# A two-layer decoder trunk on one core: two FFN chunks of layer 0 in seven products instead of eight, partial sums that stay in PSUM over a block boundary, a reordered opening of the FFN, and six row sums moved ahead

## The chip, the cores and the metric

The kernel runs on one core of a Trainium2 chip. The metric is the device time of one execution in microseconds; the profile's span goes from the first to the last instruction of one profiled execution. The engines are called PE (TensorE, matmuls; PEld is its weight load), DVE (VectorE), ACT (ScalarE), POOL (GpSimd) and SP (SyncE, which issues most transfers). Matmul results accumulate in PSUM, in eight banks of 128 x 512 floats.

## The reference, cut to what matters

The trunk has two layers over 256 tokens and 2048 channels in float32. Layer 0 mixes tokens by causal pooling, layer 1 by latent attention with 16 heads; each mixing is followed by a SwiGLU FFN with an inner width of 5632. Every sub-layer is normed, shifted, scaled and gated by vectors computed from `c`.

```python
for i in range(DEPTH):
    shift_m, scale_m, gate_m, shift_f, scale_f, gate_f = jnp.split(sc @ mod_w[i] + mod_b[i], N_MOD, axis=-1)
    ...
    x = x + gate_m[:, None, :] * y
    h = modulate(rmsnorm(x, norm_ffn[i]), shift_f, scale_f)
    x = x + gate_f[:, None, :] * swiglu(h, ffn_gate[i], ffn_up[i], ffn_down[i])

def swiglu(h, w_gate, w_up, w_down):
    return (jax.nn.silu(h @ w_gate) * (h @ w_up)) @ w_down
```

## The kernel before, in words

**Matmuls in three parts.** PE multiplies in a float32 form of less than full precision, so each operand is split into an upper half and a lower half (the rest), and a product is upper x upper + upper x lower + lower x upper. A weight tile is 512 channels by 512 columns (1 MB). `w_unit` (L389) loads one into a `raw` buffer over SP's queue; `split` (L375) makes the upper half on ACT (L380) and the lower half on DVE (L382); `proj_unit` (L397) issues the 3 parts x 4 blocks of 128 channels x 2 halves of the tokens = 24 matmuls of 128 x 512 (L405). Such a tile with its matmuls is a unit here. There are 6 `raw` buffers, 6 `hl` tiles (three pairs of halves), 8 large `act` tiles, 7 small `t2k` tiles and one `gate` tile.

**The FFN.** The 2048 channels of the hidden state are four blocks (hT[0] to hT[3]), the 5632 inner columns are eleven chunks of 512. For a chunk ("p" in `FFN_STEPS`, L59) gate and up each take four units, silu and the product make a tile of 256 tokens x 512, and it is transposed ("t"), on PE (`transposed`, L791) or, for the chunks in `TURNED_BY_DMA`, by DVE in blocks of 32 (L557) and by a write to DRAM and back on POOL's queue. Four groups of chunks (`GROUPS`) are then multiplied with the down weights ("d", `down`, L925), 12 units for three chunks, and the results are added up in x.

**Begun chunks.** Block j+1 of the hidden state isn't there when block j is. So `start_ffn` (L1072) runs chunks 0 to 5 over block 0, then 1, then 2 (three block stages; the first chunks of block 0 are in the opening), while the next block is prepared. Chunk 0 keeps its sums in PSUM (`held`); for the others `Begun.gather` (L733) copies a block's sums out (ACT, L737) or adds them to the earlier ones (DVE, L739). The last block is in the chunk's own step.

**Seven products.** In layer 1 chunks 6 to 10 (`SEVEN`) treat the first two channel blocks, the two halves of the tokens and the pair gate, up as 2 x 2 matrices of tiles and form their product in seven multiplications (`project_in_seven`, L847; matmuls at L867) of sums and differences of tiles. Differences of weight tiles are formed by `minus` (L876) on DVE in the raw buffers, before they are split. The four sums of hidden tiles are formed once per layer by `token_sums` (L808), called at the start of the first down group, and lie in an `act` and in the `gate` tile. Its parts wait in `pending`, the list of follow-up work that `flush` (L361) issues behind each split. Blocks 2 and 3 are done as usual.

**Row sums in the background.** The shift, scale and gate vectors of later steps are products of one row with a large matrix. `Part.unit` loads a 1 MB raw tile and multiplies and sums each row on DVE (L221). These units are queued in `background`; `tick` issues them at a rate set by `plan` (L354), units left over by a count of splits (`FFN0_UNITS`). In the block stages `start_ffn` pumps eight per stage. Weights in `project_in_seven` don't tick. The gate row of each FFN goes through DRAM and is spread to all partitions by POOL (L302), for layer 0 into the single `gate` tile as soon as it can; `StreamEnd.known` (L641) multiplies the sums so far with it in chunk 10's step.

**The opening.** Layer 0's vectors are needed at once and come from strip matmuls on PE (L248), one raw of 1 MB per unit, the last four from `in_mod_block`. Between them an order written out by hand (`then(n, f)`, from `n_block - 1`) sums the squares (`norm_sums`, L1235), spreads the norm (L1266), transposes the mixed stream back (`turn_of`, L1249; matmuls L1253), and picks the columns (`block.fold`, L266). The FFN's first products (L1342) follow.

The order outside the hand-written part comes from a planner that works by priority in program order; splits have priority over what stands up to 100 instructions ahead of them, and a tile is given out when its last user is done.

Of the kernel before, what the change touches and what calls it, by code (L numbers as in the profile page):

```python
# [17 lines left out]
P = 128  # L18
# [40 lines left out]
FFN_STEPS = "p0 p1 t0 p2 t1 p3 t2 p4 p5 d0 t3 t4 p6 t5 d1 p7 t6 p8 t7 p9 t8 d2 p10 t9 d3".split()  # L59
# [3 lines left out]
SEVEN = (range(0), range(6, 11))  # L63

AM, GM = 1, 2
# [4 lines left out]
LATE_GATES = ("ffn1",)  # L70
# [4 lines left out]
FFN0_UNITS, MLA_UNITS, DQ_UNITS, WO_UNITS, FFN1_UNITS = 87, 4, 6, 8, 60  # L75
DOWN_UNITS = 23

# [29 lines left out]
def tile_trunk(ctx: ExitStack, tc: tile.TileContext, a: dict, out: bass.AP):  # L107
# [176 lines left out]
    def gate_to(name, first):  # L284
# [15 lines left out]
        def load():  # L300
            gates[name] = s_row if name in LATE_GATES else gate_t([P, D])
            pool.dma_start(gates[name], row.rearrange("k q -> (k q)")[None, :].to_broadcast([P, D]))  # L302
# [324 lines left out]
    class StreamEnd:  # L627
# [13 lines left out]
        def known(self, j, tok, gate):  # L641
# [3 lines left out]
            if self.l == 0:  # L645
                dve.tensor_tensor(out=piece, in0=piece, in1=gate[:, js], op=ALU.mult)
# [71 lines left out]
    class Begun:  # L718
        def __init__(self, w, c, held):
            self.w, self.c, self.held, self.part = w[:, c], c, held, None  # L720

        def block(self, j, t_):
            if not self.held or j == 0:
                self.banks = [ps_t() for _ in range(NT)]
            hi, lo = w_unit(self.w[j])
            ends = not self.held
            proj_unit(self.banks, t_, hi, lo, ends or j == 0, ends or j == ND - 1)
            if not self.held:
                pending.append((0, lambda banks=self.banks: self.gather(banks, j)))
# [3 lines left out]
        def gather(self, banks, j):  # L733
            for tok in range(NT):
                part = self.part[:, tok, :]
                if j == 0:
                    act.activation(part, banks[tok], AF.Copy)  # L737
                else:
                    dve.tensor_tensor(out=part, in0=banks[tok], in1=part, op=ALU.add)  # L739
# [15 lines left out]
    def ffn(l, hT, gate_name, begun, then):  # L755
# [169 lines left out]
        def down(i):  # L925
            g = GROUPS[i]
            last = g[-1] == NF - 1
            if i == 0 and len(SEVEN[l]):
                release(0, DOWN_UNITS)
# [5 lines left out]
            for j in range(ND):  # L935
# [34 lines left out]
                for tok in range(NT):  # L970
                    if last:
                        pending.append((0, lambda bank=banks[tok], tok=tok, j=j: end.piece(bank, tok, j)))
                    else:
                        pending.append((0, lambda bank=banks[tok], sums=x[:, tok, js]: gather(bank, sums, i == 0)))
                        if gate_name in LATE_GATES and i == len(GROUPS) - 2:
# [3 lines left out]
        def project_chunk(c):  # L979
            if c == ASIDE:  # L980
                stream_aside(l)
            if c == NF - 1:
                end = StreamEnd(l)
                stream_end.append(end)
                for n, wait in enumerate(KNOWN):
                    pending.append((wait, lambda n=n: end.known(n // NT, n % NT, gates[gate_name])))
            if c in SEVEN[l]:
                nat[c] = project_in_seven(c)
                if c == GROUPS[-1][0]:
# [81 lines left out]

    def start_ffn(l, first, ahead, hidden, late):  # L1072
# [7 lines left out]
        with tc.issue_after(mod_ins[0].ins), tc.issue_after(hid_ins[0].ins) if hid_ins[0] else nullcontext():  # L1080
            for j in range(ND - 1):
# [4 lines left out]
                for n, (c, which) in enumerate((c, w) for c in begun for w in (GATE, UP)):  # L1086
                    if n == 2 * len(begun) - 1:
                        hT.append(hidden(j + 1, pieces))
                    if j > 0 or c >= (PAIRS if l == 0 else 1):
                        begun[c][which].block(j, hT[j])  # L1090
# [967 lines left out]
```

## Time and profile before

| | us |
|---|---|
| median of 3 runs | 1870.96 (1869.87 to 1871.59) |
| the profiled execution | 1871.2 |
| its span | 1869.4 |
| mean granted clock of PE | 0.987 |

In the profile a line such as `L405 PE MATMUL ...` is a group of instructions: source line, engine, operation, operands, count, busy time, the mean time of one in ns, and the idle time in front of them with what ended it. A row of the view by windows gives the stretch, its length, and for PE, PEld, DVE, ACT and POOL the busy time and the number of instructions, then the granted clock of PE as a share of full speed, the share of time in which the transfer engines were busy, and GB/s. The chain of waits gives start, length and what ran. A line of the timeline gives start, length, engine, line and operation, and in brackets the idle time in front with its releaser.

### The profile page before, as it was taken

Reading aid. Unit: us, or ns where it says so; the run is one execution under the profiler, and the core shown is the slowest. Engines: PE = TensorE matmul, PEld = TensorE weight load, DVE = VectorE, ACT = ScalarE, POOL = GpSimd, SP = SyncE. Lnnn points to the kernel's source line nnn. Section 1 sums busy time; section 2 is a strip of 40 time slices with the busy share of each in tenths; the row PEclk is TensorE's granted clock in tenths of the full one; section 3 lists DMA queues with packets and bytes.
Section 4 is the critical chain, followed back from the end, with each engine's and each line's share of the span. In section 5 each row is a group of like instructions: output and inputs, shape, how many; then the busy total and the mean of one; then the engine's idle time right before and its main releaser. Section 6 shows DMA issues by size and latency. Waiting matters only on the chain.

```text
span 1869.4 us, 21684 instructions
## 1 busy us (share of the span) xinstructions
PE 1821.3 (97%) x8497; PEld 1481.9 (79%) x8497; DVE 1552.1 (83%) x1552; ACT 879.4 (47%) x955; POOL 68.1 (4%) x98
## 2 busy tenths in 40 slices
PE   7779999999999999999999999999999999999998
PEld 2447888888888888888889888888888888887886
DVE  2467899999889798997798885889899887898696
ACT  3225643453433343344766735644445553655353
POOL 0000000000000000000100000100011000000000
PEclk8899999999999999999999999999999999999999
DMA  9999998889999899996495394999898587458651
GB/s 392 422 422 420 402 380 335 317 313 365 408 349 421 350 399 391 393 422 234 162 384 197 129 366 172 405 373 340 300 336 331 218 318 289 180 206 320 237 227 46
DMA packets 85192, 592.27 MB, mean 317 GB/s; under 512 B 10033, under 2 KB 10465, under 8 KB 16225
## 3 DMA queue, kind: packets, MB, share of 16 engines
q1 hardware_dynamic: 79202, 570.68, 77.9%
q0 software_dynamic: 5648, 19.93, 2.9%
q8 instruction: 66, 1.08, 0.2%
q10 hardware_dynamic: 240, 0.29, 0.0%
q14 instruction: 36, 0.29, 0.0%
HBM read 576.15 MB, written 14.70 MB: 316 GB/s over the span
## 4 chain that ended last, share of the span: by engine, by line
PE 91%; DMA 5%; DVE 2%; ACT 0%; issue 0%; SPq 0%; POOLq 0%; DVEq 0%; ACTq 0%
PE ps L405 73%; PE ps L867 4%; PE ps L415 2%; DMA raw<-in_mod_shift_dram 1%; DMA raw<-in_mod_gate_dram 1%; PE ps L248 1%; PE ps L1657 1%; PE ps L1342 1%; DMA raw<-in_mod_scale_dram 1%; DMA act<-in_pool_w_dram 1%; DVE hl L382 1%; PE ps L1743 1%; PE ps L1849 1%; DMA raw<-in_mod_block_dram 1%; PE ps L1560 1%; PE ps L1746 0%
## 5 line engine op out<-in xcount | busy, mean ns | idle before, releaser
L405 PE MATMUL ps<-hl,act 128*128 128x512 f32 x6096 | 1391.2, 389 | 0.4 <-DVE act L773 0.2
L405 PEld LDWEIGHTS ps<-hl,act 128*128 128x128 f32 x6096 | 1142.7, 188 | 238.6 <-DVE act L773 0.6
L380 ACT ACTIVATE hl<-raw 128x2048 fp32r<-128x2048 f32 x297 | 566.9, 1917 | 570.2 <-PE ps L405 279.0
L382 DVE TENSOR_TENSOR hl<-raw,hl 128x2048 fp32r<-128x2048 f32 x297 | 677.0, 2287 | 107.0 <-ACT hl L380 106.5
L221 DVE SCALAR_TENSOR_TENSOR raw<-raw,s_row 128x2048 f32<-128x2048 f32 x184 | 419.7, 2287 | 0.7 <-DMA raw<-in_mod_wt_dram 0.7
L248 PE MATMUL ps<-raw,s_strip 128*32 128x512 f32 x320 | 49.5, 710 | 28.6 <-DMA raw<-in_mod_shift_dram 16.7
L739 DVE TENSOR_TENSOR act<-ps,act 128x512 f32<-128x512 f32 x96 | 64.2, 685 | 10.2 <-PE ps L405 10.1
L867 PE MATMUL ps<-hl,act 128*128 128x512 f32 x300 | 71.6, 390 | 0.0
L867 PEld LDWEIGHTS ps<-hl,act 128*128 128x128 f32 x300 | 56.2, 188 | 11.9 <-DVE hl L382 0.2
L248 PEld LDWEIGHTS ps<-raw,s_strip 128*32 128x32 f32 x320 | 7.5, 117 | 53.1 <-issue 19.4
L415 PE MATMUL ps<-hl,act 128*128 128x512 f32 x192 | 47.6, 401 | 0.6 <-DVE act L511 0.5
L876 DVE TENSOR_TENSOR raw<-raw,raw 128x2048 f32<-128x2048 f32 x20 | 45.7, 2285 | 0.3
L415 PEld LDWEIGHTS ps<-hl,act 128*128 128x128 f32 x192 | 35.1, 188 | 10.3 <-ACT act L498 2.5
L1207 PE MATMUL ps<-act,act 128*128 128x256 f32 x128 | 34.3, 427 | 7.6 <-issue 7.6
L1207 PEld LDWEIGHTS ps<-act,act 128*128 128x128 f32 x128 | 26.9, 215 | 17.5 <-issue 13.3
L559 POOL DMA_DIRECT2D turned<-t2k x32 | 17.8, 555 | 612.6 <-DVE t2k L557 612.4
L435 ACT ACTIVATE junk<-x 128x512 bf16<-128x512 f32 x23 | 14.5, 629 | 45.7 <-DVE x L654 28.6
L528 DVE TENSOR_TENSOR hl<-raw,hl 128x2048 fp32r<-128x2048 f32 (+3 forms) x17 | 31.9, 1879 | 4.8 <-ACT hl L525 4.7
L737 ACT ACTIVATE act<-ps 128x512 f32<-128x512 f32 x32 | 18.9, 594 | 29.8 <-PE ps L405 29.8
L804 DVE TENSOR_TENSOR x<-ps,x 128x512 f32<-128x512 f32 x32 | 21.6, 690 | 12.0 <-PE ps L405 12.0
L867 PE MATMUL ps<-hl,gate 128*128 128x512 f32 x120 | 29.4, 392 | 0.6 <-ACT hl L380 0.6
L525 ACT ACTIVATE hl<-raw 128x2048 fp32r<-128x2048 f32 (+1 forms) x15 | 26.5, 1766 | 3.5 <-PE ps L405 3.5
(275 smaller groups left out, 1203.4 us busy)
## 6 DMA issues: line engine op xcount, KB each, us to landing
raw<-in_mod_wt_dram SPq DMA_DIRECT2D x152, 1024.0 KB, 8.1
raw<-in_ffn_down_dram SPq DMA_DIRECT2D x88, 1024.0 KB, 7.8
raw<-in_ffn_gate_dram SPq DMA_DIRECT2D x86, 1024.0 KB, 6.4
raw<-in_ffn_up_dram SPq DMA_DIRECT2D x86, 1024.0 KB, 6.5
raw<-in_kv_mod_wt_dram SPq DMA_DIRECT2D x32, 1024.0 KB, 8.7
raw<-in_mod_shift_dram SPq DMA_DIRECT2D x16, 1024.0 KB, 12.4
raw<-in_w_o_dram SPq DMA_DIRECT2D x16, 1024.0 KB, 6.6
raw<-in_mod_gate_dram SPq DMA_DIRECT2D x12, 1024.0 KB, 12.5
```

Of the source, the lines that this page charges most:

```text
L221: dve.scalar_tensor_tensor(out=r, in0=r, scalar=1.0, in1=s_row, op0=ALU.mult, op1=ALU.mult, accum_out=self.sums[:, self.n:self.n + 1])
L248: pe.matmul(self.bank[m * STRIP:(m + 1) * STRIP, :], lhsT=s_strip[:, self.kt + k, :], rhs=r[:, k, i, :], start=first, stop=last)
L380: hi_ins = act.activation(hi, r, AF.Copy)
L382: lo_ins = dve.tensor_tensor(out=lo, in0=r, in1=hi.bitcast(F32), op=ALU.subtract)
L405: pe.matmul(banks[tok], lhsT=t_[:, i, k, tok * P:(tok + 1) * P], rhs=w[:, k, :], start=first and n < len(part), stop=last and n >= len(ord ...
L415: pe.matmul(bank, lhsT=t_[:, i, k, tok * P:(tok + 1) * P], rhs=w[:, k, :], start=first and n == 0, stop=last and n == len(order) - 1)
L525: hid_ins[0] = act.activation(w[1], w[0], AF.Copy)
L528: dve.tensor_tensor(out=w[2][:, ks], in0=w[0][:, ks], in1=w[1][:, ks].bitcast(F32), op=ALU.subtract)
L739: dve.tensor_tensor(out=part, in0=banks[tok], in1=part, op=ALU.add)
L867: pe.matmul(bank, lhsT=a_(i, k), rhs=w[:, k, :], start=first and n == 0, stop=last and n == len(order) - 1, skip_group_check=read)
L876: dve.tensor_tensor(out=out, in0=a_, in1=b_, op=ALU.subtract)
L1207: pe.matmul(mixed[g][:, n % 2, :], lhsT=wp[g][:, k, ns], rhs=pool_all[g // 2][:, g % 2, k, :], start=k == 0, stop=k == KL - 1)
```

## The change

1. `SEVEN` gets chunks 6 and 7 of layer 0, so `token_sums` runs in layer 0 too. Its second tile takes the `gate` tile, so layer 0's gate row is loaded late, after chunk 7, and the sums are multiplied with it in the third down group as in layer 1. `FFN0_UNITS` falls from 87 to 71, since two chunks no longer tick.
2. `Begun.block` can leave a chunk's sums in PSUM over a block boundary (`goes_on`), for the chunk that comes last in a stage and first in the next; `visits` sets such orders, and the FFN starts with chunk 1 instead of 0. This holds for both layers.
3. `SOONER = 3`: three more row sums in each of the second and third block stages of layer 0.
4. In the opening the sums of squares get 64 equal columns instead of one, transposes are moved ahead, and nine transposes of the identity are added (`keep_busy`), whose results nobody reads.

```diff
-FFN_STEPS = "p0 p1 t0 p2 t1 p3 t2 p4 p5 d0 t3 t4 p6 t5 d1 p7 t6 p8 t7 p9 t8 d2 p10 t9 d3".split()
+FFN_STEPS = "p1 p0 t1 p2 t0 p3 t2 p4 p5 d0 t3 t4 p6 t5 d1 p7 t6 p8 t7 p9 t8 d2 p10 t9 d3".split()
-SEVEN = (range(0), range(6, 11))
+SEVEN = (range(6, 8), range(6, 11))
+WIDE = 64
-LATE_GATES = ("ffn1",)
+LATE_GATES = ("ffn0", "ffn1")
-FFN0_UNITS, MLA_UNITS, DQ_UNITS, WO_UNITS, FFN1_UNITS = 87, 4, 6, 8, 60
+FFN0_UNITS, MLA_UNITS, DQ_UNITS, WO_UNITS, FFN1_UNITS = 71, 4, 6, 8, 60
+SOONER = 3
...
-            gates[name] = s_row if name in LATE_GATES else gate_t([P, D])
+            gates[name] = s_row if name == "ffn1" else gate_t([P, D])
...
-        def known(self, j, tok, gate):
+        def known(self, j, tok):
             js = slice(j * CH, (j + 1) * CH)
             part, piece = self.parts[tok][:, js], x[:, tok, js]
-            if self.l == 0:
-                dve.tensor_tensor(out=piece, in0=piece, in1=gate[:, js], op=ALU.mult)
             dve.tensor_tensor(out=part, in0=piece, in1=part, op=ALU.add)
...
+            self.banks, self.empty = None, True
-        def block(self, j, t_):
-            if not self.held or j == 0:
+        def block(self, j, t_, goes_on=False):
+            first, ends = self.banks is None, j == ND - 1 or not (self.held or goes_on)
+            if first:
                 self.banks = [ps_t() for _ in range(NT)]
             hi, lo = w_unit(self.w[j])
-            ends = not self.held
-            proj_unit(self.banks, t_, hi, lo, ends or j == 0, ends or j == ND - 1)
-            if not self.held:
-                pending.append((0, lambda banks=self.banks: self.gather(banks, j)))
+            proj_unit(self.banks, t_, hi, lo, first, ends)
+            if ends and not self.held:
+                pending.append((0, self.gather))
                 if j == ND - 1:
                     flush()
-        def gather(self, banks, j):
+        def gather(self):
             for tok in range(NT):
                 part = self.part[:, tok, :]
-                if j == 0:
+                if self.empty:
-                    act.activation(part, banks[tok], AF.Copy)
+                    act.activation(part, self.banks[tok], AF.Copy)
                 else:
-                    dve.tensor_tensor(out=part, in0=banks[tok], in1=part, op=ALU.add)
+                    dve.tensor_tensor(out=part, in0=self.banks[tok], in1=part, op=ALU.add)
+            self.banks, self.empty = None, False
...
-            if i == 0 and len(SEVEN[l]):
-                release(0, DOWN_UNITS)
+            if i == 0:
+                if l == DEPTH - 1:
+                    release(0, DOWN_UNITS)
                 token_sums()
...
-                        if gate_name in LATE_GATES and i == len(GROUPS) - 2:
+                        if i == len(GROUPS) - 2:
...
-                if c == GROUPS[-1][0]:
+                if c == min(SEVEN[l][-1], GROUPS[-1][0]):
                     late_gates.pop()()
...
+    def visits(j, n):
+        return ([*range(n)], [n - 1, *range(3, n - 1), 0, 1, 2], [*range(2, n), 0, 1])[j]
...
                 todo = KD // 2 if j + 1 >= ND - late else 0
-                for n, (c, which) in enumerate((c, w) for c in begun for w in (GATE, UP)):
+                if l == 0 and j > 0:
+                    todo += SOONER
+                for n, (c, which) in enumerate((c, w) for c in visits(j, len(begun)) for w in (GATE, UP)):
...
-                        begun[c][which].block(j, hT[j])
+                        begun[c][which].block(j, hT[j], n >= 2 * len(begun) - 2)
...
-                    pe.matmul(total[:, tok:tok + 1], lhsT=squares[n][:, k, tok * P:(tok + 1) * P], rhs=ones[:, 0:1],
+                    pe.matmul(sums_wide[:, tok, :], lhsT=squares[n][:, k, tok * P:(tok + 1) * P], rhs=ones[:, :WIDE],
                               start=n + tok + k == 0, stop=n + tok + k == 4)
...
+    def keep_busy(n):
+        for _ in range(n):
+            pe.transpose(total[:, :P], ident, ident)
...
     then(n_block, norm_sums, (1, 2))
+    then(n_block, turn_of, ORDER[1])
     then(n_block, lambda: pairs[1].split_upper())
     then(n_block, turned_copies)
     then(n_block, norm_rows)
     then(n_block, lambda: pairs[1].split_lower())
-    then(n_block + 1, turn_back, ORDER[1])
     then(n_block + 1, norm_spread)
     then(n_block + 1, parts_of_first)
-    then(n_block + 2, turn_back, ORDER[2])
-    then(n_block + 3, turn_of, last, (0,))
+    then(n_block + 1, turn_back, ORDER[2])
+    then(n_block + 2, turn_of, last, (0,))
+    then(n_block + 2, keep_busy, 4)
+    then(n_block + 3, turn_of, last, (1,))
     then(n_block + 3, block.fold)
-    then(n_block + 3, turn_of, last, (1,))
+    then(n_block + 3, keep_busy, 5)
```

## The prediction on record

> **What bounds the kernel now.** I read the page first, then the chain of waits in order of time, then the busy time by stage.
>
> ```profile
> span 1869.4 us, 21684 instructions
> PE 1821.3 (97%) x8497; PEld 1481.9 (79%) x8497; DVE 1552.1 (83%) x1552; ACT 879.4 (47%) x955; POOL 68.1 (4%) x98
> DVE  2467899999889798997798885889899887898696
> DMA  9999998889999899996495394999898587458651
> PE 91%; DMA 5%; DVE 2%; ACT 0%; issue 0%; SPq 0%; POOLq 0%; DVEq 0%; ACTq 0%
> L405 PE MATMUL ps<-hl,act 128*128 128x512 f32 x6096 | 1391.2, 389 | 0.4 <-DVE act L773 0.2
> L382 DVE TENSOR_TENSOR hl<-raw,hl 128x2048 fp32r<-128x2048 f32 x297 | 677.0, 2287 | 107.0 <-ACT hl L380 106.5
> L221 DVE SCALAR_TENSOR_TENSOR raw<-raw,s_row 128x2048 f32<-128x2048 f32 x184 | 419.7, 2287 | 0.7 <-DMA raw<-in_mod_wt_dram 0.7
> L739 DVE TENSOR_TENSOR act<-ps,act 128x512 f32<-128x512 f32 x96 | 64.2, 685 | 10.2 <-PE ps L405 10.1
> ```
>
> PE is 91% of the chain that ended last, and its largest group waited 0.4 us in all. So an instruction taken off PE shortens the run, provided the others keep up; a matmul's 389 ns is its latency, since they are pipelined. The 5% of DMA in the chain is the opening. The engine next to the bound is DVE. Its prices are busy time over count: 677.0/297 = 2.28 us for a lower half of a weight tile (L382), 419.7/184 = 2.28 for a row sum (L221), 64.2/96 = 0.67 for a 128x512 add.
>
> **Part 1: fewer products.** Layer 1 of this same kernel already forms chunks 6 to 10 this way, so its chunk 6 shows what the new order costs PE. From the chain of waits, and the busy time of the whole chunk 6 and of chunk 9 in layer 1:
>
> ```profile
> 1478.98 2.72 PE ps L867 x12
> 1481.70 5.44 PE ps L405 x24
> 1479.00:1520.00 41.00, 41.00 (x182) 33.89 (x182) 34.18 (x17) 24.47 (x19) 0.00 (x0) 1.00 0.62 234
> 1667.00:1708.00 41.00, 40.21 (x176) 32.47 (x175) 38.08 (x26) 23.53 (x19) 2.63 (x4) 1.00 0.59 213
> ```
>
> A product is 12 matmuls, 2.72 us. An ordinary chunk has four channel blocks times gate and up times 24 = 192 matmuls; the new order has seven products for the first two blocks, 84, and 96 for the other two: 180. Two chunks save 2 x 2.72 = **5.4 us**, if PE stays fed. The first row of windows says it can be: PE busy 41.00 of 41.00. The second says that it isn't always: DVE is at 38.08 of 41, and PE loses 0.8 us.
>
> **Part 2: the opening.** The chain of waits just before the FFN, with the clock in three windows, the wide-to-be sums, a transfer's landing and the issue of the block strips:
>
> ```profile
> 138.61 12.45 DMA raw<-in_mod_block_dram
> 151.10 1.93 PE ps L248 x8
> 153.03 1.90 PE ps L1253 x8
> 154.93 0.85 PE ps L1266 x2
> 155.78 1.51 PE ps L248 x8
> 157.29 1.02 PE ps L1253 x8
> 158.32 1.04 PE ps L248 x8
> 160.09 1.07 PE ps L266 x8
> 162.09 22.10 PE ps L1342 x96
> 147.22 2.84 PE L1239 MATMUL ps<-ones,t2k 128*128 128x1 f32 x24
> 150.00:152.00 2.00, 0.96 (x9) 0.20 (x8) 1.08 (x4) 1.48 (x3) 0.70 (x1) 0.50 0.98 406
> 154.00:156.00 2.00, 2.00 (x11) 1.26 (x13) 0.18 (x1) 1.20 (x2) 0.00 (x0) 0.50 1.00 418
> 158.00:160.00 2.00, 1.90 (x15) 0.66 (x13) 0.00 (x0) 1.56 (x3) 0.00 (x0) 1.00 1.00 418
> 148.60 1.91 ACT L1325 ACTIVATE hl<-raw 128x2048 fp32r<-128x2048 f32 x1 [0.40 <-DMA raw<-in_ffn_first_dram]
> L236 SPq DMA_DIRECT2D raw<-in_mod_block_dram x4: 328/328/328, 132.8 to 142.7; - x4
> ```
>
> After 24 one-column matmuls and a wait the granted clock is 0.50, and eight strip matmuls take 1.93 us where they take 1.04 at full clock. The change makes the sums 64 columns wide, puts eight transposes (ORDER[1]) into the wait of about 1 us that ends at 151.10, and adds nine transposes as filler. If the clock holds, the three strip units and the transposes between 151.10 and 159.36 shrink from 8.3 us to about 6. What then ends last is a transfer. Strip raws landed at 151.06 (138.61 + 12.45) and a weight raw at 148.60, one megabyte each 2.5 us; the last strip, third from 151.06 counting itself, so lands at 151.06 + 2 x 2.5 = 156.1 (an estimate: landings of the last two aren't shown). It was used at 158.32. Gain 0 to **2.2 us**; I take 2.2, for the DMA queue is full in all three windows (0.98 to 1.00) and its order up to there is unchanged. The 64-column sums cost between nothing (a weight load in 0.118 us, 2.84/24, is there already) and as much again, 2.8; either fits ahead of 156.1, except for what hangs on it on DVE. The filler stands in PE's own waits, 162.09 - 161.16 = 0.9 us after the fold for five transposes.
>
> [...]
>
> **Part 3: DVE and the row sums.** Chunk 5, then 2, then 1 stay in their banks over a block boundary. That takes 3 x 4 adds off DVE in the second and third block stages of layer 0 (chunk 5's first gather, on ACT, falls one stage later). In come six row sums. Later in the FFN DVE gets: six row sums fewer; four times tile sums with halves, 14 operations of 0.67; per chunk three more lower halves, four differences of weight tiles, five adds more. The gate's eight multiplications only move, from chunk 10 to the third down group. The stages before:
>
> ```profile
> 227.80:358.60 130.80, 130.80 (x579) 108.31 (x578) 120.91 (x113) 55.59 (x43) 0.00 (x0) 1.00 0.91 349
> 358.60:842.80 484.20, 484.20 (x2166) 401.19 (x2165) 435.17 (x353) 194.72 (x140) 8.62 (x13) 1.00 0.95 380
> 358.60:426.30 67.70, 67.70 (x312) 56.33 (x311) 65.91 (x65) 32.37 (x31) 0.00 (x0) 1.00 0.83 310
> 426.30:493.50 67.20, 67.20 (x306) 55.68 (x305) 60.54 (x48) 26.89 (x23) 0.71 (x1) 1.00 0.98 398
> 453.57 27.25 PE ps L405 x120
> 454.36 1.92 ACT L380 ACTIVATE hl<-raw 128x2048 fp32r<-128x2048 f32 x1 [0.48 <-ACT t2k L293]
> ```
>
> Second and third block stage: 120.9 + 6 x 2.28 - 12 x 0.67 = 126.6 of 130.8 us, 97%; DMA 349 + 6.3 MB/130.8 us = 397 GB/s. FFN up to the last down group: 435.2 - 13.7 + 14 x 0.67 + 2 x (7 x 2.28 + 5 x 0.67) = 435.2 - 13.7 + 9.4 + 38.6 = 469.5 of 484.2 - 5.4 = 478.8 us, **98%** against 90% before. PE never waits in these rows, so the change can win nothing there beyond the products; it can lose.
>
> Where first? In the first down group (426.3 to 493.5), which had 60.5 of 67.2. The rate of row sums goes from 84/87 to 78/71 a unit, so 12 units carry 1.6 more, 3.6 us; the six chunks before, full at 65.9 of 67.7, push their own 3.6 into it; the tile sums add 9.4. That makes 77.1, 9.9 too many. Two things absorb it. The margin: the upper half made at 454.36 to 456.28 is taken by the second unit from 453.57, at 453.57 + 27.25/5 = 459.0, 2.7 us later (counting units through the ring of three tile pairs). And chunk 6 carries no row sums: 34.2 of 41.0, 6.8 us free into which late row sums can slip, since nobody waits for them soon. The loss is 9.9 - 2.7 = 7.2 if none slips, 0.4 if all does. I take **2.6**: most slips, as row sums are the work that the planner lets fall behind, but each holds one of six raw buffers, which weights then lack, and chunk 9 of layer 1 lost 0.8 at a smaller load.
>
> Costed at nothing: the gate row's load on POOL's queue, now behind chunk 7, lands over 80 us before the third down group uses it, and behind it only stores of turned blocks wait; uncovered it would be one landing. Chunk 1 before chunk 0 and the transposes with them: PE has the same units. Layer 1's changed visits: PE is busy throughout its blocks too. Six row sums' transfers on SP's queue go ahead of weights that the 397 GB/s still leave room for.
>
> Sum, on the profiled execution (1871.2 us, span 1869.4, 1.8 around it): 1871.2 - 5.4 - 2.2 + 2.6 = 1866.2. The median 1870.96 is 0.2 lower: **1866.0 us**. 0.2% of it, about what a measurement can tell from no change, is 3.7 us.
>
> **The rivals.**
> *DVE takes it back.* If few row sums slip, PE loses the full 7.2 there, and perhaps a little again in the third down group, which gains the eight multiplications: 1871.0 - 7.6 + 7.2 = 1870.6, up to 1872. For it: 98% over 479 us; 97% was held for 68 us only. Against it: the surplus of work lies in one place, with slack behind it.
>
> *Tile sums come too late: slower.* They need two t2k tiles at a time; of seven, chunks 3, 4 and 5 hold six until the transposes of chunk 3, at 480.8 in this trace (the 27.25 us from 453.57 end there), one or two units before chunk 6. If they run only then, in front of the lower halves that PE needs, the third product of chunk 6 waits for all 9.4 us of them and for two differences and two lower halves behind, 4 x 2.28 = 9.1: 1871.0 - 7.6 + 9.4 + 9.1 = 1881.9 if none of it is beside PE's work, 1875 with 7 us beside it. It decides from where more than 8.2 + 5.4 us of DVE work (36 matmuls of chunk 6 and the last unit before) stands ahead of that product's tile. Against: only three of the four sums lead to that product, and layer 1 does it without a wait; but there turned chunks go out by DMA early and t2k is free.
>
> *The clock stays down.* Transposes between strips may not hold it, or the strips are too sparse: at 0.50 three strip units take 0.9 us more each than I allow, which eats the 2.2: 1868.2.
>
> **How the numbers follow.** Forecast (1862.5 to 1867.3: all of the 2.2, loss 0 to 4) 0.52; clock stays down 0.12; DVE takes it back 0.18; tile sums late 0.18. That the products aren't fewer is excluded by the list of chunks. Faster than 1867.3: the forecast's 0.52 and 0.03 of the clock's case, 0.55; slower than 1874.7: most of the last, 0.16; same 0.29. The range leaves out the worse half of the last case and little below: 1862 to 1876.
>
> **What would show it.** Right: 24 matmuls fewer over L405 and L867 together; FFN products (L1342) beginning near 160 at clock 1.00 throughout; DVE near 97% from 230 to 840; one or two PE gaps between 430 and 540. Wrong: PE waiting for DVE or ACT by more than 7 us in layer 0; a clock under 1 at 155; PE idle ahead of the first product over a tile sum; or no wait at all, and 1863.

## The result, and the profile after

The changed kernel takes 1886.58 us (median of 5 runs, 1885.54 to 1888.79) against 1870.96 (1869.87 to 1871.59): ratio 1.0086, interval [1.0076, 1.0097]. It is slower by 16 us where 5 were forecast as a gain. From the page of the profiled execution (1888.79 us):

```profile
span 1887.0 us, 21675 instructions
PE 1822.4 (97%) x8482; PEld 1477.3 (78%) x8482; DVE 1581.1 (84%) x1566; ACT 894.6 (47%) x973; POOL 67.8 (4%) x98
PE 83%; DVE 9%; DMA 4%; issue 2%; ACT 1%; POOL 0%; SPq 0%; DVEq 0%; POOLq 0%; ACTq 0%
L408 PE MATMUL ps<-hl,act 128*128 128x512 f32 x5904 | 1356.3, 391 | 8.3 <-ACT hl L383 6.7
L385 DVE TENSOR_TENSOR hl<-raw,hl 128x2048 fp32r<-128x2048 f32 x303 | 688.7, 2284 | 107.0 <-ACT hl L383 106.6
```

L405 of before is L408, L382 is L385, L867 is L870. PE has its fewer matmuls, and its largest group now waits 8.3 us instead of 0.4. DVE's share of the chain has gone from 2% to 9%, and it is there that the chain must be read: most of PE's waits name ACT, whose upper half came late because of DVE. The waits of PE that are new or longer, from the view of waits (what waited for what, in all, how often, the longest):

```profile
PE ps L408 <- ACT hl L383: 6.7, 5, 2.8
PE ps L294 <- DVE cols L308: 2.7, 1, 2.7
PE ps L870 <- ACT hl L383: 1.8, 3, 1.0
PE ps L870 <- DVE gate L822: 1.6, 1, 1.6
PE ps L408 <- DVE hl L385: 1.4, 3, 0.7
```

These are 14.2 us, all but 0.8 of them in layer 0's FFN, and two of the pauses cost more than their length: at 2.72 us for 12 matmuls, those behind 2.67 us (88 in 21.82) took 1.9 us longer, those behind 2.84 us (24 in 8.54) 3.1. Where they are, from PE's timeline (start, length, line, count, and in brackets the wait ahead):

```profile
413.01 5.73 PE L408 MATMUL ps<-hl,act 128*128 128x512 f32 x24 [1.40 <-ACT hl L383]
421.41 0.27 PE L294 MATMUL ps<-con,cols 128*16 128x128 f32 x1 [2.67 <-DVE cols L308]
421.43 21.82 PE L408 MATMUL ps<-hl,act 128*128 128x512 f32 x88
...
500.42 1.91 PE L794 MATMUL ps<-con,t2k 128*128 128x128 f32 x16
502.09 3.12 PE L870 MATMUL ps<-hl,act 128*128 128x512 f32 x12
...
508.04 8.54 PE L408 MATMUL ps<-hl,act 128*128 128x512 f32 x24 [2.84 <-ACT hl L383]
...
520.04 2.12 PE L870 MATMUL ps<-hl,gate 128*128 128x512 f32 x8 [1.55 <-DVE gate L822]
...
618.70 2.88 PE L870 MATMUL ps<-hl,act 128*128 128x512 f32 x12
...
815.54 27.51 PE L408 MATMUL ps<-hl,act 128*128 128x512 f32 x120 [1.99 <-ACT hl L383]
```

Behind the waits of chunk 6, 24 matmuls take 8.54 us, where 24 take 5.44 at full clock: the granted clock is 0.50 from 508 to 514 us. By stage, in the changed kernel and then in the one before (columns as in the prediction):

```profile
358.00:426.00 68.00, 62.95 (x277) 50.15 (x276) 62.87 (x62) 27.09 (x27) 0.00 (x0) 0.97 0.87 332
426.00:493.00 67.00, 66.29 (x293) 54.40 (x292) 64.61 (x50) 27.87 (x21) 0.00 (x0) 1.00 0.96 386
493.00:560.00 67.00, 61.69 (x268) 49.46 (x267) 59.46 (x49) 37.58 (x33) 0.00 (x0) 0.95 0.61 239
```

```profile
358.00:426.00 68.00, 68.00 (x314) 56.56 (x313) 65.90 (x65) 32.67 (x30) 0.00 (x0) 1.00 0.83 311
...
493.00:560.00 67.00, 67.00 (x302) 55.55 (x301) 57.03 (x44) 27.14 (x18) 2.62 (x4) 1.00 0.93 362
```

For all kernels below one length is compared, "the FFN length": from the first FFN products (L1342 before, L1357 after) to the last down products, which a chain of waits shows as 44 matmuls. Before and after:

```profile
877.16 9.98 PE ps L415 x44
```

```profile
161.41 22.10 PE ps L1357 x96
...
894.27 9.98 PE ps L418 x44
```

Before it is 877.16 - 162.09 = 715.1 us, after 894.27 - 161.41 = 732.9. The products take 5.4 off, so 23.2 us are lost in layer 0's FFN; ahead of it the changed profile is 0.7 us quicker, and behind it 0.5 slower. Up to chunk 6's first product it is 502.09 - 161.41 = 340.7 against 493.5 - 162.09 = 331.4, so 9.3 in the begun chunks and the first down group. From there to chunk 7's first product it is 116.6; 180 + 288 matmuls of 2.72/12 us and eight transposes (0.88) make 107.0, so 9.6 in chunk 6. The remaining 4.3 come later: the two longest waits there are 0.96 us in chunk 7 and 1.99 us in chunk 10 (at 815.54), and what makes up the rest stays open.

DVE's own line in chunk 6 shows the cause there (DVE's timeline):

```profile
450.46 0.68 DVE L826 TENSOR_TENSOR t2k<-act,act 128x512 f32<-128x512 f32 x1
...
495.68 0.17 DVE L276 TENSOR_TENSOR cols<-sums,vcol 128x16 f32<-128x16 f32 x1
501.06 0.69 DVE L827 TENSOR_TENSOR t2k<-act,act 128x512 f32<-128x512 f32 x1 [5.21 <-PE ps L794]
501.67 2.28 DVE L385 TENSOR_TENSOR hl<-raw,hl 128x2048 fp32r<-128x2048 f32 x1
```

The first operation of the tile sums runs at 450.46; the second, of the same sum, needs another `t2k` tile, which chunk 3 gives back only at its transposes, at 500.42, now behind all twelve units of the down group. DVE stands idle for 5.21 us, and the lower halves of chunk 6 behind that instruction stand with it.

### The profile page after: what moved, and what is told of

Same layout as the page of the kernel before. It is cut to its first block, busy times and chain, and to the rows that moved or that the text cites. A ratio compares the mean times of both kernels' runs of the same rounds, so it can differ in the third digit from the quotient of the medians.

```text
span 1887.0 us, 21675 instructions
## 1 busy us (share of the span) xinstructions
PE 1822.4 (97%) x8482; PEld 1477.3 (78%) x8482; DVE 1581.1 (84%) x1566; ACT 894.6 (47%) x973; POOL 67.8 (4%) x98
## 4 chain that ended last, share of the span: by engine, by line
PE 83%; DVE 9%; DMA 4%; issue 2%; ACT 1%; POOL 0%; SPq 0%; DVEq 0%; POOLq 0%; ACTq 0%
PE ps L408 64%; PE ps L870 6%; DVE hl L385 4%; DVE raw L224 2%; PE ps L418 2%; DMA raw<-in_mod_shift_dram 1%; DMA raw<-in_mod_wt_dram 1%; PE ps L1357 1%; PE ps L251 1%; DMA raw<-in_mod_scale_dram 1%; PE ps L1675 1%; PE ps L1761 1%; PE ps L1867 1%; DMA raw<-in_mod_gate_dram 1%; ACT hl L383 1%
## 5 line engine op out<-in xcount | busy, mean ns | idle before, releaser
L408 PE MATMUL ps<-hl,act 128*128 128x512 f32 x5904 | 1356.3, 391 | 8.3 <-ACT hl L383 6.7
L408 PEld LDWEIGHTS ps<-hl,act 128*128 128x128 f32 x5904 | 1109.0, 188 | 244.1 <-ACT hl L383 8.8
L383 ACT ACTIVATE hl<-raw 128x2048 fp32r<-128x2048 f32 x303 | 577.5, 1916 | 529.7 <-PE ps L408 225.6
L385 DVE TENSOR_TENSOR hl<-raw,hl 128x2048 fp32r<-128x2048 f32 x303 | 688.7, 2284 | 107.0 <-ACT hl L383 106.6
L870 PE MATMUL ps<-hl,act 128*128 128x512 f32 x420 | 101.4, 391 | 1.0 <-ACT hl L383 1.0
L870 PEld LDWEIGHTS ps<-hl,act 128*128 128x128 f32 x420 | 78.3, 188 | 18.4 <-ACT hl L383 1.4
L879 DVE TENSOR_TENSOR raw<-raw,raw 128x2048 f32<-128x2048 f32 x28 | 63.9, 2284 | 0.4
L741 DVE TENSOR_TENSOR act<-ps,act 128x512 f32<-128x512 f32 x80 | 52.9, 681 | 10.9 <-PE ps L408 10.8
L870 PE MATMUL ps<-hl,gate 128*128 128x512 f32 x168 | 41.8, 395 | 3.1 <-DVE gate L822 1.6
L870 PEld LDWEIGHTS ps<-hl,gate 128*128 128x128 f32 x168 | 31.2, 188 | 11.2 <-DVE gate L822 2.0
```

The costliest lines, as they stand in the source:

```text
L383: hi_ins = act.activation(hi, r, AF.Copy)
L385: lo_ins = dve.tensor_tensor(out=lo, in0=r, in1=hi.bitcast(F32), op=ALU.subtract)
L408: pe.matmul(banks[tok], lhsT=t_[:, i, k, tok * P:(tok + 1) * P], rhs=w[:, k, :], start=first and n < len(part), stop=last and n >= len(ord ...
L741: dve.tensor_tensor(out=part, in0=self.banks[tok], in1=part, op=ALU.add)
L870: pe.matmul(bank, lhsT=a_(i, k), rhs=w[:, k, :], start=first and n == 0, stop=last and n == len(order) - 1, skip_group_check=read)
L879: dve.tensor_tensor(out=out, in0=a_, in1=b_, op=ALU.subtract)
```

## The experiments

Unless it is said otherwise an edit is made to the changed kernel. Ratios are to the kernel before, measured beside each run. The questions come in this order: are the seven products needed for the loss, what holds up chunk 6, what holds up the begun chunks, and can the loss be avoided. "Row sums a unit" means row sums issued per weight tile that ticks.

| run | median us | ratio [95%] | FFN length us |
|---|---|---|---|
| e1_beside | 1869.72 | 0.9995 [0.9986, 1.0005] | 715.1 |
| e2_turned | 1884.22 | 1.0069 [1.0052, 1.0086] | 729.8 |
| e3_early_turn | 1881.33 | 1.0054 [1.0039, 1.0069] | 726.9 |
| e4_half_rows | 1886.12 | 1.0079 [1.0064, 1.0094] | 730.3 |
| f1_sooner | 1878.93 | 1.0040 [1.0026, 1.0054] | 724.7 |
| f2_rate | 1883.65 | 1.0066 [1.0051, 1.0081] | 730.5 |
| f3_both | 1882.39 | 1.0059 [1.0044, 1.0074] | 727.8 |
| f4_early_late | 1884.93 | 1.0072 [1.0057, 1.0087] | 729.7 |
| g1_spread | 1901.82 | 1.0165 [1.0149, 1.0180] | 719.2 |
| g2_one_chunk | 1886.61 | 1.0082 [1.0065, 1.0099] | 714.7 |
| g3_gate_later | 1878.43 | 1.0039 [1.0025, 1.0054] | 724.6 |
| g4_six_ahead | 1910.08 | 1.0209 [1.0193, 1.0224] | 730.0 |
| h1_one_even | 1872.30 | 1.0007 [0.9998, 1.0017] | 718.3 |
| h2_gate_row | 1880.52 | 1.0048 [1.0031, 1.0065] | 727.2 |
| h3_gate_row_only | 1869.62 | 0.9993 [0.9984, 1.0002] | 715.6 |
| h4_two_even | 1880.59 | 1.0052 [1.0037, 1.0067] | 727.4 |
| i2_other_engines | 1973.35 | 1.0551 [1.0529, 1.0573] | - |
| i4_other_engines_plain | 1954.22 | 1.0447 [1.0431, 1.0463] | - |

**Without the seven products, and what they bring along.**

```diff
-SEVEN = (range(6, 8), range(6, 11))
+SEVEN = (range(0), range(6, 11))
-LATE_GATES = ("ffn0", "ffn1")
+LATE_GATES = ("ffn1",)
-FFN0_UNITS, ... = 71, ...
+FFN0_UNITS, ... = 87, ...
-SOONER = 3
+SOONER = 0
```

(and no token sums in layer 0.)

> The changed kernel without the seven products in layer 0 and what goes with them (no tile sums there, gate row loaded early, 87 units, no row sums moved ahead); the opening, the banks kept over a block boundary and the order of chunks stay. All theories that put the loss on the seven products (DVE over-subscribed, tile sums late, raw buffers held) say the same: no PE gap in layer 0 after the opening, and 1870.96 minus the 0.7 us by which the first products came sooner, 1869 to 1871. If the kept banks or the new order of chunks cost something themselves, it is above 1873.

The 16 us are gone, so the opening, the order of visits and the banks kept over a boundary do no harm; the chain of waits has its FFN products early:

```profile
159.71 22.05 PE ps L1358 x96
```

That is 2.4 us sooner than before, in a profiled execution that is 1.0 us below the run's median. The time is no different from before within its interval.

**Chunk 6: who holds the tiles.** Two runs free `t2k` tiles earlier, by turning chunks 3 to 5 by DMA (`TURNED_BY_DMA = (range(3, 9), ...)`), and by a step of its own that transposes chunk 3 into PSUM ahead of the down group:

```diff
-p4 p5 d0 t3 t4 p6
+p4 p5 u3 d0 t3 t4 p6
```

> Chunks 3, 4 and 5 of layer 0 are turned by DVE blocks and transfers as in layer 1, not by PE: their t2k tiles are free early, DVE has six more 128x512 operations (4 us), PE 24 transposes fewer (2.6 us). Tile sums late: chunk 6's loss falls to 1 to 3 us, total 1875 to 1879. DVE over-subscribed: 4 us more for DVE eat what the freed tiles give, 1883 to 1888.

> Chunk 3 is transposed into PSUM before the first down group and copied out after it, so its two t2k tiles are free when the tile sums start; the same instructions on every engine. Tile sums late: chunk 6 loses 1 to 3 us instead of 10, total 1877 to 1880. DVE over-subscribed alone: DVE only gets back the 5.2 us in which it stood behind the transposes, and the sums move into the down group, 1881 to 1885. Raw buffers held: no change, 1885 to 1888.

Windows of the second:

```profile
358.00:426.00 68.00, 62.91 (x277) 50.10 (x276) 64.53 (x64) 28.74 (x28) 0.00 (x0) 0.97 0.86 325
460.00:500.00 40.00, 37.79 (x164) 30.34 (x163) 39.90 (x36) 18.03 (x16) 0.00 (x0) 1.00 0.98 384
500.00:520.00 20.00, 18.62 (x83) 14.46 (x83) 19.90 (x13) 12.37 (x12) 0.00 (x0) 1.00 0.48 186
```

DVE's wait of 5.21 us is gone and 5.2 us of the time with it. From chunk 6's first product (502.68) to chunk 7's (612.08) it is 109.4 us, so chunk 6 loses 2.4 instead of 9.6; but PE now waits 2.2 us for lower halves in the down group, where the sums run. The loss in the begun chunks (62.91 of 68) is untouched: it is another one. The first run, which gives DVE six more operations, wins back 2.4 us: chunk 6 loses less there too (PE 64.50 of 67 from 493 to 560, against 61.69), but the begun chunks and the down group lose more (61.66 of 68, 64.51 of 67).

**Is it DVE's amount of work?** Each background row sum on half of its columns, the other half left out:

```diff
+cs = slice(0, D // 2 if self in background or self.brief else D)
-dve.scalar_tensor_tensor(out=r, in0=r, scalar=1.0, in1=s_row, ...
+dve.scalar_tensor_tensor(out=r[:, cs], in0=r[:, cs], scalar=1.0, in1=s_row[:, cs], ...
```

> Row sums of the background multiply and sum only half of each row (1024 of 2048 columns), so 168 of them cost DVE about 1.2 us instead of 2.3, with the same transfers and raw buffers; the vectors they give are wrong. DVE over-subscribed: the gaps in the six begun chunks go (9 us) and some of chunk 6's, 1873 to 1878. Tile sums late: chunk 6 keeps most of its 10 us, since the wait is for PE's transposes, 1876 to 1880. Raw buffers or transfers: no change, 1885 to 1888.

```profile
358.00:426.00 68.00, 64.32 (x287) 50.74 (x286) 58.18 (x68) 29.67 (x30) 0.00 (x0) 1.00 0.81 308
```

DVE is busy 58.2 us of 68, and PE still loses 3.7. The timeline of DVE there shows why:

```profile
349.72 0.08 DVE L227 DVE_READ_ACCUMULATOR raw<-raw,s_row 128x1 f32 x1
358.49 0.69 DVE L744 TENSOR_TENSOR gate<-ps,gate 128x512 f32<-128x512 f32 x1 [8.68 <-PE ps L411]
359.09 2.28 DVE L388 TENSOR_TENSOR hl<-raw,hl 128x2048 fp32r<-128x2048 f32 x1
```

The waits of PE in this stretch name lower halves of DVE alone (2.4 us), and none a transfer, though the total lies where the rival of raw buffers and transfers had it. DVE waits 8.68 us for PE with an addition (L744 here, L741 in the changed kernel) at the head of its line, and the next lower half, which needs nothing of PE, stands behind it. The number of lower halves ahead of such operations can be read off the program's DVE order: ahead of the up multiplications of the six begun chunks there are 36, 38, 40, 42, 44, 46 before and 34, 36, 38, 41, 43, 45 after. And beside them go 8 row sums before, 11 after. In this run the order is not quite that of the changed kernel (34, 36, 38, 40, 42, 44). In chunk 6 nothing is won at all: DVE stands 7.34 us in front of the second operation of the tile sums, and from 493 to 560 PE has 60.63 us of 67. So the amount of work alone explains neither place.

**What costs it: the six ahead, or the rate?** Three runs on the kernel of the first experiment: `SOONER = 3` alone, `FFN0_UNITS = 76` alone, and `SOONER = 3` with 71.

> The changed kernel without seven products (chunks 6 and 7 as before, early gate row, no token sums), row sums again spread over 87 units, but three more row sums in each of the second and third block stages. Theory L (lead): what PE loses in the six begun chunks is set by how many lower halves stand ahead of each up multiplication in DVE's order. In DVE's program order the first multiplication of the six chunks has 36, 38, 40, 42, 44, 46 lower halves ahead of it before, 34, 36, 38, 41, 43, 45 after, and 35, 36, 38, 41, 43, 46 here: so a part of the loss, 1 to 5 us between 358 and 426, total 1870 to 1875. Rival T (throughput): what counts is DVE's work in that stretch, which here is lower than before (0.90 row sums a unit instead of 0.97): no loss, total 1868 to 1870.

> As the run beside it, but with the six row sums where they were and the row sums at 84 in 76 units, 1.1 a unit like in the changed kernel. Theory L: 36, 37, 39, 42, 43, 46 lower halves ahead of the up multiplications, one fewer than before in three places: 0 to 1.5 us lost between 358 and 426, total 1869 to 1872. Rival T: DVE's work in that stretch rises from 63.7 us by 0.14 x 24 x 2.2 = 7 us above the 68 us there are: 3 to 7 us lost, total 1873 to 1877.

> Both together: six row sums ahead and 1.1 a unit, still no seven products and no token sums. DVE's order up to the end of the six begun chunks is then that of the changed kernel (34, 36, 38, 41, 43, 45 lower halves ahead). Theory L: the changed kernel's whole loss in that stretch, 7 to 10 us, total 1876 to 1880, and no further loss behind it. Rival S (the seven products themselves, through transfers or buffers of chunk 6, hold up the chunks before): no loss, total 1869 to 1871.

PE's timeline in the first and in the second, and the window of the third:

```profile
404.65 19.89 PE L408 MATMUL ps<-hl,act 128*128 128x512 f32 x87
431.85 0.38 PE L294 MATMUL ps<-con,cols 128*16 128x128 f32 x1 [7.32 <-DVE cols L308]
431.88 13.46 PE L408 MATMUL ps<-hl,act 128*128 128x512 f32 x49
```

```profile
445.76 0.27 PE L294 MATMUL ps<-con,cols 128*16 128x128 f32 x1 [3.52 <-DVE cols L308]
445.79 19.57 PE L408 MATMUL ps<-hl,act 128*128 128x512 f32 x78
...
529.07 16.19 PE L408 MATMUL ps<-hl,act 128*128 128x512 f32 x64 [2.54 <-ACT hl L383]
```

```profile
358.00:426.00 68.00, 62.89 (x278) 50.16 (x277) 63.68 (x63) 27.89 (x28) 0.00 (x0) 0.97 0.86 326
```

The third reproduces the loss of the begun chunks without any seven products (62.89 against 62.95), so it isn't theirs; its total is above both ranges, as PE loses another 2.4 us between 680 and 860. The first two went past both theories (and rival T counts 24 units in a stretch of twelve, so its price is twice too high). With the six alone there is one wait, of 7.32 us: `spread` transposes the gate row on PE, for the last of the gate's sixteen row sums, which now falls where DVE is latest; 49 matmuls behind it take 13.46 us instead of 11.1. With the rate alone (1.1 a unit) the begun chunks run full, and the loss follows, mostly between 430 and 760: 15.4 us of the FFN length, more than the 12.7 of both together.

**The gate row.** A first attempt (`pending.append((5, spread))` for `(1, spread)`, on f1_sooner) left layer 0's order as it was, since the list is emptied at the end of each begun chunk; it is a repetition of that run. The second moves one row sum, the gate's last, behind eight of the next vector:

```diff
     kv_part(0, shift_to, C_SKV)
+    background.insert(-8, background.pop(-KD - 1))
```

> The kernel without seven products and with three more row sums in each of two block stages (1878.9), with one edit: the spread of the gate row, a transpose on PE that waited 7.3 us for the last of its row sums, is issued four splits later in PE's order. Theory H (head of the line): the 7.3 us are PE's own order, behind which matmuls stood that were ready; with the transpose later the wait and the slow clock behind it go: 1869 to 1872. Rival: DVE is late as a whole by then, and PE waits instead for lower halves: 1874 to 1879.

> The same move of one row sum in the kernel without seven products and with three more row sums in each of two block stages (1878.9; one wait of 7.3 us and matmuls 2.4 us slower behind it). Theory H: both go, 1869 to 1871. Rival B: PE waits for lower halves instead, 1875 to 1879.

> The changed kernel with chunk 3 turned early (1881.3), and the last of the sixteen row sums of layer 0's gate row done after eight sums of the next vector, so that its transpose on PE comes later. Theory H (a single late sum at the head of PE's line): its wait of 2.7 us and the slow clock behind it go, 1876 to 1879. Rival B (DVE is late as a whole): PE waits elsewhere for as long, 1880 to 1883.

Moved in the kernel with the six ahead (h3_gate_row_only), it takes all of the 9 us away:

```profile
358.00:426.00 68.00, 68.00 (x313) 56.56 (x312) 63.51 (x61) 29.15 (x27) 0.00 (x0) 1.00 0.85 323
```

So, at this rate, the six row sums ahead cost nothing by themselves, nor do the one or two lower halves less ahead. In the changed kernel with chunk 3 turned early, the same move (h2_gate_row) changes next to nothing (1880.52 against 1881.33; FFN length 727.2 against 726.9): the wait of 2.6 us goes, but PE then waits for the halves behind, as a DVE that is late as a whole would have it.

**Fewer row sums a unit.** f4_early_late has chunk 3 turned early and `SOONER = 0` (84 in 71 units, 1.18). Three others spread them thinner. On top of that, g1_spread has `MIX_LATE = 18` (six left to layer 1), two units of each seven-product chunk that tick, and 79 units; g2_one_chunk has one chunk only, `MIX_LATE = 15` and 83 units; g4_six_ahead is g1_spread with `SOONER = 3` and the `(5, spread)` that had no effect in layer 0.

> The changed kernel with seven products in chunks 6 and 7, with chunk 3 turned ahead of the first down group, and with the six row sums left where they were (84 over 71 units). 36, 37, 39, 41, 43, 46 lower halves ahead of the up multiplications. Theory L: of the 8.7 us in the six begun chunks 6 to 8 go, against 1881.3 with the six row sums ahead; behind them the denser row sums (1.18 a unit) cost 0 to 3: total 1873 to 1878. Rival T: the chunks carry 0.08 x 24 x 2.2 = 4 us more of row sums, the loss grows: 1882 to 1886.

> The changed kernel with chunk 3 turned early, the six row sums where they were, six row sums left to layer 1's mixing, the rest spread over four more units at the end of the FFN and four units inside chunks 6 and 7: 78 in 79 units, 0.99 a unit. Theory B (backlog): DVE clears about 0.97 row sums a unit beside the lower halves, as in the kernel before; whatever is issued beyond that stands in front of lower halves and of the gate row's transposes until it has been paid, so at 0.99 the loss goes and the 5.4 us of the products remain: total 1864 to 1869. Rival K: chunks 6 and 7 are too full by themselves (their halves, differences and now two row sums each): 3 to 7 us lost in 500 to 550 and 600 to 660 together, total 1870 to 1875.

> As the run beside it, but only chunk 6 in seven products: 81 row sums in 83 units, 0.98 a unit, three left to layer 1's mixing, none in chunk 6. Theory B: half of the products' gain, no loss: total 1866 to 1869. Rival K: the loss in chunk 6 alone, 2 to 4 us: 1869 to 1872.

> As the first of this call, but with the six row sums ahead in the block stages (72 left in 79 units, 0.91 a unit) and the gate row's transpose four splits later. Theory B: the six are paid in the block stages, which have DVE at 60 to 62 of 66 us, so nothing is lost: 1864 to 1869. Rival L: DVE enters the six begun chunks with one lower half less ahead, which costs 2 to 5 us there: 1867 to 1873.

At 1.18 the begun chunks lose only 1.1 us, but the next 67 us lose 7.3: the loss moved. The first down group of f4_early_late:

```profile
426.00:493.00 67.00, 59.71 (x256) 48.37 (x254) 63.97 (x59) 26.88 (x25) 0.00 (x0) 0.95 0.96 371
```

At 0.99 (g1_spread) PE is full in both stages (68.00 of 68 and 67.00 of 67). With the six ahead at 0.91 a unit (g4_six_ahead) the gate row's wait is back, and it is the only one in these two stages:

```profile
PE ps L294 <- DVE cols L308: 8.2, 1, 8.2
```

The FFN length is 719.2 in g1_spread; with one chunk it is 714.7. These runs are slower as a whole all the same: the row sums left over are then issued in four units of layer 1's mixing, where PE has 25 us of 40, with transfers at 1.00:

```profile
940.00:980.00 40.00, 25.07 (x114) 21.39 (x113) 37.48 (x39) 13.62 (x18) 0.00 (x0) 0.75 1.00 406
```

More were left over than meant: nothing ticks in the last down group (`hold`), so units counted there never came. What g1_spread still loses in the FFN, 719.2 - (715.1 - 5.4) = 9.5 us, lies mostly in chunks 6 and 7, where PE has 37.35 of 40 us and 56.92 of 60: here rival K was right. In chunk 6 (L891 is `minus`, L882 the product; timelines of DVE, ACT and PE):

```profile
499.94 2.29 DVE L891 TENSOR_TENSOR raw<-raw,raw 128x2048 f32<-128x2048 f32 x1
...
502.33 5.52 ACT L383 ACTIVATE hl<-raw 128x2048 fp32r<-128x2048 f32 x3 [5.29 <-DVE raw L891]
...
504.29 2.12 PE L882 MATMUL ps<-hl,act 128*128 128x512 f32 x8 [1.47 <-ACT hl L383]
```

A weight difference is formed on DVE, then its upper half on ACT, then PE has it: in a seven-product chunk what stands ahead in DVE's line delays ACT too.

**Without leaving work to layer 1.** Row sums may run into the first half of the last down group:

```diff
-                if last and j == 0:
+                if last and j == (2 if l == 0 else 0):
                     hold()
```

with one chunk, chunk 3 turned early, `SOONER = 0` and 83 units (h1_one_even), and with both, the gate's sum moved, `SOONER = 3` and 75 units (h4_two_even).

> Only chunk 6 in seven products, chunk 3 turned early, no row sums ahead, nothing left to layer 1: row sums may run on into the first half of the last down group, 84 in 83 units, 1.01 a unit. Theory B (row sums beyond what DVE clears beside the lower halves stand in front of work that PE needs): layer 0's FFN, from its first product to the last down sums, takes 713 to 716 us against 715.1 before, total 1867 to 1871. Rival R (1.01 is already too dense, as 1.1 was): 3 to 8 us more: 1872 to 1877.

> The changed kernel with chunk 3 turned early, the last gate sum moved, and row sums that may run on into the first half of the last down group: 78 in 75 units, 1.04 a unit. Theory B: the loss in the six begun chunks and the first down group falls from about 9 us to 2 to 5: total 1870 to 1876. Rival L (the order at the entry of the begun chunks, 34, 36, 38, 41, 43, 45 lower halves ahead, is unchanged): the loss stays, 1877 to 1881.

One chunk at 1.01 a unit is at the time of before (its FFN 3.2 us longer, the opening 1.8 shorter), so the product it saves is lost again, as rival R had it. Both at 1.04 are 12.3 us longer in the FFN, so they lose 17.7, as much as h2_gate_row: the begun chunks lose less (PE 65.62 of 68 against 63.38), but the last down group, into which row sums now run, loses 3.3 us (36.70 of 40 from 860 to 900). No version beat the kernel before by more than its interval.

**Row sums on other engines.** Every fourth row sum as a multiplication on POOL and a sum on ACT:

```diff
+if self in background and self.n % 4 == 1:
+    pool.tensor_tensor(out=r, in0=r, in1=s_row, op=ALU.mult)
+    act.activation(r, r, AF.Copy, accum_out=self.sums[:, self.n:self.n + 1])
```

> Seven products in chunks 6 and 7, chunk 3 turned early, the last gate sum moved, no row sums ahead, and every fourth row sum formed by a multiplication on POOL and a sum on ACT instead of on DVE: 21 of 84 fewer for DVE, 46 us, of 478. Theory B (DVE's work as such): the loss in the six begun chunks and the first down group goes, chunks 6 and 7 keep 2 to 4 us of theirs: 1866 to 1871. Rival P: a multiplication of 128x2048 on POOL takes long (an estimate from its 128x512 operation of 1.76 us: 7 us), holds its raw buffer and is waited for by ACT, in whose line the upper halves stand: 1876 to 1890.

> The same in the kernel without seven products and without row sums ahead (1869.7), as a control: theory B sees DVE relieved where it was no bound: 1868 to 1871. Rival P: the same waits of ACT for POOL, 1874 to 1890.

The first is 102 us slower than the kernel before, and the control loses most of that too, 83 us; both are far above either expectation. The control's groups, and DVE and POOL side by side:

```profile
L225 POOL TENSOR_TENSOR raw<-raw,s_row 128x2048 f32<-128x2048 f32 x42 | 232.1, 5525 | 767.9 <-DMA raw<-in_mod_wt_dram 527.0 <-DMA raw<-in_kv_mod_wt_dram 112.9 <-DVE soft L1797 59.4
L389 DVE TENSOR_TENSOR hl<-raw,hl 128x2048 fp32r<-128x2048 f32 x297 | 736.5, 2489 | 174.8 <-ACT hl L387 173.2 <-issue 1.2
```

```profile
357.66 5.93 POOL L225 TENSOR_TENSOR raw<-raw,s_row 128x2048 f32<-128x2048 f32 x1 [36.18 <-DMA raw<-in_mod_wt_dram]
...
360.06 7.88 DVE L389 TENSOR_TENSOR hl<-raw,hl 128x2048 fp32r<-128x2048 f32 x2 [0.94 <-ACT hl L387]
```

POOL takes 5.5 us, and the lower halves that meet it here end late: the pair takes 7.88 us, where two took 4.49 in f1_sooner (at 409.40). POOL ends at 363.59, two lower halves of 2.2 later it is 368.0, and the pair ends at 367.94. ACT, in turn, waits 191 us in all for POOL's products, as rival P had it. How the 83 us divide between the two isn't shown. So this is no test of DVE's load, and that question stays open on this side.

## Why the prediction was wrong

**The products: right.** 24 fewer matmuls over L408 and L870, 5.4 us, and chunk 6 in layer 1 at the old pace.

**The opening: about right.** FFN products begin at 161.41 in this profile, and between 159.6 and 161.0 in the experiments, against 162.09: 0.7 to 2.5, forecast 2.2. The clock is 1.00 from 150 to 162 in the windows of the changed kernel and to 160 in those of the first experiment, so the rival that it stays down fell. The fillers didn't bring it up: the first of them starts at 156.97. Whether the wide sums did it alone (24 in 2.89 us, against 2.84 before, so their width cost nothing) or with the transposes moved behind them, no run here separates.

**The step that failed is the loss term of part 3: 2.6 us taken, 23 found in the same FFN.** The amount of work was right: 469.5 us of DVE forecast up to the last down group, and 469.5 busy between 358 and 860 us. What failed is the step from there to PE's loss, that most of the surplus would slip into free time: the stretch took 502 us, not 478.8. Three things in it were wrong.

First, "most slips, as row sums are the work that the planner lets fall behind". The program fixes the order on an engine (in chunk 6 DVE stood 5.21 us in front of one operation, the lower halves behind it), and with 11 row sums instead of 8 beside the begun chunks they stood ahead of lower halves, one or two fewer of which were ready. I let the six begun chunks push their excess on without cost; they cost most of the 9.3 us, the down group, where I had placed the loss, about 1. Shown are: that it comes without seven products (f3_both), that neither of the two causes alone loses anything there but the gate row's wait (h3_gate_row_only, f2_rate up to 426), and that, with the six left in their place, thinning the row sums from 1.18 to 0.99 a unit takes away all that the begun chunks and the first down group lose (8.4 us, f4_early_late against g1_spread). How it divides between amount and order isn't shown: with half the amount, in nearly the same order, 3.7 us were still lost (e4_half_rows).

Second, a row sum that nobody waits for soon: the last one of the gate row is waited for at once, by a transpose in PE's line. That is 2.7 us here and 7.3 in f1_sooner, and no rival had it. Here its removal won nothing clear (h2_gate_row), as PE then waited for lower halves.

Third, the rival "tile sums come too late" came true as described: `t2k` tiles of chunk 3, sums only behind its transposes, 9.6 us lost in chunk 6, where I gave 11.6 to 18.5. Its argument against, that only three of four sums lead to that product, was no help, since DVE waits in the middle of the first. e3_early_turn shows it: with the tiles free, chunk 6 loses 2.4 us, and 5.2 of the whole come back, since the sums then take 2.2 us from the down group. I gave it 0.18 and priced it without the loss before it.

Two smaller errors. Every pause was priced by its length; but matmuls behind some pauses ran at a lower granted clock first: 0.50 from 508 to 514 us, which cost 3.1 us in chunk 6 beside waits of 5.1, and 0.83 from 420 to 440 us in f1_sooner, where 49 matmuls took 2.4 us longer behind the 7.3. And the forecast's lower bound, 1862.5, is 0.9 below what its own terms give (1871.0 - 5.4 - 2.2 = 1863.4).

## What to carry to other kernels

On an engine that is 90% busy, ask of each added instruction what stands behind it in the order, not what share of the time it adds: its margin is the number of finished tiles ahead of the consumer, and two causes that each leave some of it can together take it all. Look for instructions that wait for a buffer or for another engine at the head of a full line, and for small ones on the bounding engine (a transpose of one row) that follow background work. Work moved out of a full stage needs a named stage with room for its transfers too.

## What the runs showed of the hardware

In the control with POOL (i4_other_engines_plain) two lower halves that began at 360.06, inside a POOL multiplication from 357.66 to 363.59, took 7.88 us instead of 4.49 and ended 4.35 us behind it; the row sum that began ahead of it, at 356.83, took 2.28 as elsewhere. Over the whole run, with 42 multiplications of 5.5 us, the means of three DVE groups rose against e1_beside: lower halves from 2.286 to 2.489 us (297 of them), row sums from 2.284 to 2.530 (184 there, 142 here), differences of weight tiles from 2.285 to 2.499 (20). Other groups kept theirs: additions with an operand in PSUM took 0.679 us against 0.682 (80) and 0.684 against 0.687 (32), transposes in blocks of 32 took 0.695 against 0.694 (32). How many operations of each group began inside a multiplication these means don't say, so what sets the groups apart isn't shown.

After pauses of 2.5 to 7.3 us PE's next 24 to 88 matmuls took 0.25 to 0.36 us each on average instead of 0.227 (2.72/12), in the changed kernel (24 behind 2.84 us, 88 behind 2.67), f1_sooner (49 behind 7.32) and f2_rate (78 behind 3.52, 64 behind 2.54). In the changed kernel the granted clock was 0.50 from 508 to 514 us behind the 2.84 us and 1.00 from 514 to 520, and 0.50 from 423 to 425 behind the 2.67 us and 1.00 from 427 to 430. In f1_sooner it was 0.83 from 420 to 440 us, where the 7.32 us end, and 1.00 from 440 to 460; that run's FFN length is 9.6 us above before (724.7 against 715.1). The length of a pause alone didn't decide it here: behind 1.99 us in the changed kernel the clock was 1.00 from 815 to 822 us, and with a pause of 2.3 us in e4_half_rows 1.00 from 420 to 440 (PE busy 17.64 of 20), while with one of 1.8 us in g1_spread it was 0.97 from 620 to 640 (PE 18.18 of 20) and 0.94 from 640 to 660.
